# The first unit of the leading tiles by token halves, with two of five token blocks loaded behind the first conditioning and weights

## The chip, the core and the metric

The kernel runs on one core of a Trainium2 chip. The metric is the device time of one execution in microseconds. Before the change it is 2295.79 us, the median of three runs (2294.99, 2295.79 and 2299.85).

A core has a tensor engine (PE, with its weight loads shown as PEld), a vector engine (DVE), a scalar engine (ACT), GpSimd (POOL) and SyncE (SP), which here only issues transfers. Each engine runs its own instructions in the order in which they stand in its queue. Transfers between HBM and on-chip memory run on 16 DMA engines; most are issued by SP, the first four token tiles by ACT and the small rows by POOL.

## The reference

Two layers of a diffusion trunk are run for 512 latent tokens and 128 context tokens, 640 rows of width 2048 together. Each layer normalises its input, applies a shift and a scale per feature that come from a condition vector, projects the result, mixes, projects back and adds a gated residual. The part that the change touches is the start of the first layer:

```python
m = jax.nn.silu(cond) @ w + b                                # ada_w: 2048 x 6144 for each layer
y = xf * lax.rsqrt(jnp.mean(xf * xf, axis=-1, keepdims=True) + EPS)
hs = rms_norm(xs, norm_g[layer]) * (1.0 + sc_s) + sh_s       # latent tokens, condition c
hp = rms_norm(xp, norm_g[layer]) * (1.0 + sc_p) + sh_p       # context tokens, condition c_ctx
h @ w_in                                                     # 2048 x 6656 in the even layer
```

## The kernel before

Activations are kept with features on the 128 partitions and the 640 tokens along the free axis; `h` has 16 feature tiles. Each is held as a rounded part and a remainder (`hi`, `lo`), and each weight tile as `wh` and `wl`; a product is three matmuls (L256 to L258 of the profile): `wh*hi`, `wh*lo`, `wl*hi`. A matmul covers 320 tokens, one *token half* (`HV`): half 0 is tokens 0 to 319, half 1 is 320 to 639, whose last 128 are the context tokens.

**The start.** The tokens come as five blocks of 128 rows, each in two tiles `xb` of 1024 features (L101): blocks 0 and 1 through ACT's queue, blocks 2 to 4 through SP's. `x_block` (L878) transposes a block in four groups of four PE transposes (L884) into PSUM; DVE copies three of the groups and ACT the fourth into `xT` (L885), and ACT sums the squares of the block (L889). GpSimd takes the inverse root. `x_rows` (L895) spreads the inverse roots of the tokens over all partitions with one matmul a block (L899), and ACT copies them into `rows` (in `tables`, L900). Small rows (norm gains, biases, convolution weights, condition vectors) are loaded as `rows_a` and `rows_b` and turned by two transposes (L127, L128) into one PSUM tile; `sT`, the condition on partitions, is read from it. PSUM tiles for all of these come from two buffers (`psT`).

**Conditioning.** `ada_on_pe` (L163) computes two feature tiles of the shift or scale: two transfers of 1 MB (`ada`, L170, four buffers), 16 matmuls (L173), a copy on ACT (L176), two transposes (L179), a reduction on DVE (L181) and the bias (L161); a scale is then combined with the norm gain (L149).

**Leading tiles.** `run_tiles` begins with eight output tiles of the projection, the *leads*, while the conditioning still arrives. The inner dimension is taken in eight *units* of two feature tiles. A unit loads the weights of the eight leads (128 KB each, `load_raw`, L233, four buffers), rounds them on ACT (L220) and takes the remainder on DVE (L221), makes `h` (L922, then L926 on ACT and L927 on DVE) and runs 96 matmuls. Two leads keep their sum in PSUM through all units; the other six (`TRANS`) go through one pair of PSUM buffers and are copied (first unit, L349, ACT) or added (later, L351, DVE) into `sum`. After the first lead of a unit `ahead` issues the next unit's scale and shift.

The order in which the engines' instructions stand is set by a scheduler that starts from the program's order, and by the buffers of the pools: an instruction that needs a buffer waits for the last reader of what was in it.

Of the kernel before, what the change touches and what calls it, by code (L numbers as in the profile page):

```python
# [20 lines left out]
P = 128  # L21
D = 2048
KT = D // P
NS = 512
# [26 lines left out]
def trunk_kernel(ctx: ExitStack, tc: tile.TileContext, I: dict, O: dict):  # L51
# [12 lines left out]
    def psT():  # L64
        return pT.tile([P, 512], F32, tag="T", name="T")
# [37 lines left out]


    nc.sync.dma_start(rows_a[0:16, :], I["c"].rearrange("b (k p) -> (b k) p", p=P))
# [20 lines left out]
    t0 = psT()  # L126
    PE.transpose(t0[:, 0:112], rows_a[0:112, :], ident[0:112, 0:112])  # L127
    PE.transpose(t0[:, 128:205], rows_b[0:77, :], ident[0:77, 0:77])  # L128
    V.tensor_scalar(sT[:, :, 0:2], t0[:, 0:32].rearrange("p (c k) -> p k c", c=2), 0.5, None, ALU.mult)
    V.tensor_copy(vec[:, 0:80], t0[:, 32:112])  # L130
    V.tensor_copy(vec[:, 80:157], t0[:, 128:205])
    norm_g = [vec[:, 0:16], vec[:, 16:32]]
# [29 lines left out]

    def ada_on_pe(l, cb, h=0, n=4):  # L163

        acc, m, wd = psT(), 16 // n, n * P
        for kt in range(KT):
            if kt % m == 0:
                w = ada_t[0].rearrange("p (k n) -> p k n", k=m)
                ada_t.append(ada_t.pop(0))
                nc.sync.dma_start(w, I["ada_w"][l, kt * P:(kt + m) * P, cb * 512 + h * 256:cb * 512 + h * 256 + wd]  # L170
                                  .rearrange("(k p) n -> p k n", p=P))
            g = kt % 4
            PE.matmul(acc[32 * g:32 * g + 32, 0:wd], sT[:, kt, :], w[:, kt % m, :],  # L173
                      start=(kt < 4), stop=(kt >= KT - 4), tile_position=(0, 32 * g))
        sb = ada_sb
        A.copy(sb[:, 0:wd], acc[:, 0:wd])  # L176
# [131 lines left out]
    def slot(fill=None, rate=0.0, attend=True):  # L308
# [4 lines left out]
        while credit[0] >= 1.0:  # L313
            next(fill, None)
            credit[0] -= 1.0

    def run_tiles(jobs, w_ap, make_h, fill=None, rate=0.0, ahead=None, order=(0, 1, 2, 3), before=None,
                  last=None, by_half=False, mid=False, trans=[], grace=0, cut=None, summed=None, led=None, freed=None):
        if trans:
# [12 lines left out]
        units = [(pos, qd, js) for pos, qd in enumerate(order) for js in (cut or [(0, 4)])]  # L332
        for ui, (pos, qd, js) in enumerate(units):
            raws = {n: load_raw(w_ap, jobs[n][0], qd, js) for n in leads[:W_BUFS]}
            parts = {n: split_w(raws[n]) for n in raws}
# [537 lines left out]
    xT = [t[:, 0:4 * NT].rearrange("p (j t) -> p j t", j=4) for t in xTm]  # L873
    rx = sp.tile([P, 5], F32, name="rx")

    rows = tables[:, 0:NT]

    def x_block(b, ts):  # L878
        s4 = small.tile([P, 2], F32, tag="s4", name="s4")
        for g in range(4):  # L880
            ta = psT()
            for j in range(4):
                o = g % 2 * 512 + j * P
                PE.transpose(ta[:, j * P:(j + 1) * P], ts[g // 2][:, o:o + P], ident)  # L884
            (A.copy if g == 3 else V.tensor_copy)(xT[g][:, :, b * P:(b + 1) * P],  # L885
                                                  ta.rearrange("p (j t) -> p j t", j=4))
            if g % 2 == 0:
                junk = pS.tile([P, 1024], F32, tag="S", name="sqj")
# [29 lines left out]
    def h0_maker(k):  # L918
        x = xT[k // 4][:, k % 4, :]
        t = h_t[k % 2]  # L920
        for sl, c in TOKS:
            V.scalar_tensor_tensor(out=t[:, sl], in0=x[:, sl], scalar=gsc[0][:, k, c:c + 1], in1=rows[:, sl],  # L922
                                   op0=ALU.mult, op1=ALU.mult)
        hi, lo = new_h(k)
        for sl, c in TOKS:
            A.activation(hi[:, sl], t[:, sl], AF.Identity, bias=mod[0][:, k, c:c + 1])  # L926
# [131 lines left out]
    for i in range(4, 8):  # L1058
        b_tiles(i)

    u0, c0, b0, h0, g0, g1 = jobs[4:10]
    jobs[0:10] = [u0, c0, jobs[0], jobs[1], g0, jobs[2], jobs[3], g1, b0, h0]
    run_tiles(jobs, I["ev_w_in"][0], h0_maker, fill0, FILL0, ada_group, trans=TRANS, grace=GRACE, cut=((0, 2), (2, 4)),
              summed=keep, led=even_start, freed=ada_start)
    drain(prep)
# [604 lines left out]
```

## Time and profile before

| what | value |
|---|---|
| median of three runs | 2295.79 us |
| profiled execution, device time | 2294.4 us |
| its span, first to last instruction | 2292.6 us |
| PE busy | 2255.9 us (98%) |
| DVE / ACT / POOL busy | 1589.8 / 1088.9 / 160.0 us |
| bytes moved | 342.89 MB, mean 150 GB/s |
| granted clock of the tensor engine | 0.999 |

The page lists busy time by engine, then 40 slices of the span, the DMA queues, the chain of work that ended last, and groups of instructions by line with mean duration and the idle time ahead of them. Other views are instructions in order of time, waits, and the busy time of each engine in chosen stretches. An ended wait is put down to the signal that came last. Matmuls overlap: one of 320 columns is shown as 0.31 us, and the next begins 0.15 us after it.

### The profile page before, as it was taken

The numbers are of one execution on the slowest core, as the hardware profiler recorded it, in microseconds if no ns is written. First come the engines' busy times: TensorE is split into PE (matmuls) and PEld (weight loads), VectorE is DVE, ScalarE is ACT, GpSimd is POOL, SyncE is SP. The second block draws the span as 40 slices with busy tenths as digits, with TensorE's granted clock in tenths as the row PEclk, the third lists the DMA queues.
The fourth block names the chain that finished last, engine by engine and source line by source line (L and its number), as shares of the span: only waits on it lengthen the run. The fifth ranks groups of instructions, "written<-read, shape, count | busy, mean of one in ns | idle before, by whom it ended". The sixth has DMA issues, their size and how long they took to land.

```text
span 2292.6 us, 41100 instructions
## 1 busy us (share of the span) xinstructions
PE 2255.9 (98%) x15900; PEld 2178.0 (95%) x15900; DVE 1589.8 (69%) x2831; ACT 1088.9 (47%) x2304; POOL 160.0 (7%) x224
## 2 busy tenths in 40 slices
PE   7999999999999999999999999999999999999999
PEld 5889999999999999999999999999999999999999
DVE  4666968779779776887787665365665655557775
ACT  5325652443522222544464443465565676755443
POOL 1001000000000000000100001011111100000101
PEclk9999999999999999999999999999999999999999
DMA  9985537547367564854553335223223221238642
GB/s 321 294 270 161 158 113 218 152 133 219 116 210 216 177 191 137 277 173 140 164 155 108 116 118 152 79 60 104 79 63 101 71 60 49 76 101 269 184 138 62
DMA packets 380899, 342.89 MB, mean 150 GB/s; under 512 B 16402, under 2 KB 338416, under 8 KB 380192
## 3 DMA queue, kind: packets, MB, share of 16 engines
q1 hardware_dynamic: 366288, 296.00, 43.0%
q0 software_dynamic: 13696, 42.10, 5.4%
q8 instruction: 125, 2.05, 0.4%
q10 hardware_dynamic: 720, 2.16, 0.3%
q14 instruction: 70, 0.57, 0.1%
HBM read 301.27 MB, written 38.93 MB: 148 GB/s over the span
## 4 chain that ended last, share of the span: by engine, by line
PE 85%; DVE 4%; ACT 4%; DMA 3%; issue 3%; POOL 1%; SPq 0%; ACTq 0%; POOLq 0%; DVEq 0%
PE pq L537 7%; PE pq L536 7%; PE pq L535 7%; PE pa L256 6%; PE pa L257 6%; PE pb L256 6%; PE pa L258 6%; PE pb L257 6%; PE pb L258 6%; PE pb L271 2%; PE pb L270 2%; PE pa L270 2%; PE pb L272 2%; PE pa L272 2%; PE pa L271 2%
## 5 line engine op out<-in xcount | busy, mean ns | idle before, releaser
L220 ACT ACTIVATE wh<-raw 128x512 fp32r<-128x512 f32 (+1 forms) x456 | 273.1, 600 | 574.0 <-PE pb L257 406.9
L221 DVE TENSOR_TENSOR wl<-raw,wh 128x512 fp32r<-128x512 f32 (+1 forms) x456 | 295.7, 650 | 212.3 <-ACT wh L220 191.9
L256 PE MATMUL pa<-h,wh 128*128 128x320 f32 x1024 | 325.3, 319 | 4.3 <-ACT h L220 2.0
L257 PE MATMUL pa<-h,wh 128*128 128x320 f32 x1024 | 319.5, 313 | 1.7 <-DVE h L221 0.8
L258 PE MATMUL pa<-h,wl 128*128 128x320 f32 x1024 | 318.2, 311 | 0.9 <-DVE wl L221 0.9
L257 PE MATMUL pb<-h,wh 128*128 128x320 f32 x1024 | 317.1, 310 | 0.0
L258 PE MATMUL pb<-h,wl 128*128 128x320 f32 x1024 | 316.8, 309 | 0.0
L256 PE MATMUL pb<-h,wh 128*128 128x320 f32 x1024 | 316.6, 310 | 0.0
L198 DVE SCALAR_TENSOR_TENSOR acc<-adaw,sT,acc 128x1024 f32<-128x1024 f32 x240 | 299.7, 1276 | 0.0
L256 PEld LDWEIGHTS pa<-h,wh 128*128 128x128 f32 x1024 | 193.1, 189 | 18.3 <-issue 10.0
L257 PEld LDWEIGHTS pa<-h,wh 128*128 128x128 f32 x1024 | 193.3, 189 | 7.6 <-issue 3.3
L535 PE MATMUL pq<-h,wh 128*128 128x320 f32 x640 | 198.7, 311 | 0.4 <-ACT wh L220 0.4
L537 PE MATMUL pq<-h,wl 128*128 128x320 f32 x640 | 198.0, 309 | 0.1
L536 PE MATMUL pq<-h,wh 128*128 128x320 f32 x640 | 197.7, 309 | 0.0
L258 PEld LDWEIGHTS pa<-h,wl 128*128 128x128 f32 x1024 | 193.1, 189 | 3.5 <-issue 2.1
L257 PEld LDWEIGHTS pb<-h,wh 128*128 128x128 f32 x1024 | 192.2, 188 | 1.0 <-issue 0.8
L256 PEld LDWEIGHTS pb<-h,wh 128*128 128x128 f32 x1024 | 192.1, 188 | 0.8 <-issue 0.4
L258 PEld LDWEIGHTS pb<-h,wl 128*128 128x128 f32 x1024 | 192.3, 188 | 0.0
L537 PE MATMUL pq<-T,wl 128*128 128x320 f32 x480 | 147.7, 308 | 0.2 <-DVE wl L221 0.2
L536 PE MATMUL pq<-T,wh 128*128 128x320 f32 x480 | 147.9, 308 | 0.0
L535 PE MATMUL pq<-T,wh 128*128 128x320 f32 x480 | 147.6, 308 | 0.1
L270 PE MATMUL pa<-h,wh 128*128 128x320 f32 x432 | 141.0, 326 | 0.0
(431 smaller groups left out, 5306.0 us busy)
## 6 DMA issues: line engine op xcount, KB each, us to landing
adaw<-in_ada_w SPq DMA_DIRECT2D x128, 512.0 KB, 4.3
raw<-in_ev_w_in SPq DMA_DIRECT2D x176, 256.0 KB, 3.5
raw<-in_od_w_in SPq DMA_DIRECT2D x160, 256.0 KB, 2.9
ada<-in_ada_w SPq DMA_DIRECT2D x32, 1024.0 KB, 7.9
w<-in_od_w_in SPq DMA_DIRECT2D x24, 512.0 KB, 4.0
yd<-y POOLq DMA_DIRECT2D x32, 320.0 KB, 3.2
yin<-yd SPq DMA_DIRECT2D x32, 320.0 KB, 4.5
w<-yd SPq DMA_DIRECT2D x32, 320.0 KB, 4.2
```

The lines of the kernel that those rows point to most:

```text
L198: V.scalar_tensor_tensor(out=acc[c], in0=w, scalar=sT[:, kt, c:c + 1], in1=acc[c], op0=ALU.mult, op1=ALU.add)
L220: A.activation(hi, x, AF.Copy)
L221: V.tensor_sub(lo, x, hi)
L256: PE.matmul(ps, wh[:, i, :], hi[:, sl], start=(j == js[0] if alone else (pos == 0 and j == 0)), stop=False)
L257: PE.matmul(ps, wh[:, i, :], lo[:, sl], start=False, stop=False)
L258: last_mm[0] = PE.matmul(ps, wl[:, i, :], hi[:, sl], start=False, stop=(j == js[1] - 1 if alone else (pos == 3 and j == 3)))
L270: PE.matmul(ps, wh[:, j, :], hi[:, sl], start=(qd == 0 and j == 0), stop=False)
L271: PE.matmul(ps, wh[:, j, :], lo[:, sl], start=False, stop=False)
L272: PE.matmul(ps, wl[:, j, :], hi[:, sl], start=False, stop=(qd == 3 and j == 3))
L535: PE.matmul(ps, wh[:, j, :], hi, start=(new and h == 0 and j == 0), stop=False, **kw)
L536: PE.matmul(ps, wh[:, j, :], lo, start=False, stop=False, **kw)
L537: PE.matmul(ps, wl[:, j, :], hi, start=False, stop=(h == 1 and j == 3), **kw)
```

## The change

Four things are done.

- Only blocks 0 to 2 are loaded at the beginning. `first_loads` then issues the first unit's two scale tiles, the weights of leads one and two (both in one buffer, `first_raws`), the two shift tiles, the other six leads' weights in three buffers, and behind them blocks 3 and 4. It transposes blocks 0 to 2, computes scale, the norm rows of three blocks, and shift.
- `first_unit` runs the first unit by token halves: `h` of both feature tiles for half 0, the eight leads with 24 + 24 matmuls, then the same for half 1. The six leads with sums alternate between two PSUM buffers by their number, and each half is copied by ACT.
- `between` puts the transposes of block 3 behind the third lead of half 0, those of block 4 behind the sixth, `rows_b` behind the seventh, and the two missing norm rows behind the eighth. Squares of blocks 3 and 4 are taken in four quarters on ACT into an SBUF tile, as the PSUM tile that held them before is one of the leads' sums now. The block's transposes are held behind the last matmul ahead of them.
- The transpose of `rows_a` and `rows_b` is split: the 32 rows of the condition first, `rows_a` behind block 0, `rows_b` late.

The amount of data and of arithmetic stays, but for one transpose more and eight quarter squares in place of four.

```diff
-    xs = [x_load(b) for b in range(5)]
+    xs = [x_load(b) for b in range(3)]
...
-    PE.transpose(t0[:, 0:112], rows_a[0:112, :], ident[0:112, 0:112])
-    PE.transpose(t0[:, 128:205], rows_b[0:77, :], ident[0:77, 0:77])
+    PE.transpose(t0[:, 0:32], rows_a[0:32, :], ident[0:32, 0:32])
...
+    def first_unit(raws, leads, trans, pps, make_h, ahead, units, between):
+        pos, qd, js = units[0]
+        parts = {}
+        for i, raw in enumerate(raws):
+            wh, wl = split_w(raw)
+            for j in range(2):
+                parts[leads[2 * i + j]] = wh[:, j], wl[:, j]
+        for half_i, sl in HV:
+            for k in range(*js):
+                make_h(k, half_i)
+            for i, n in enumerate(leads):
+                if half_i and n == leads[1]:
+                    ahead(*units[1][1:])
+                if n in trans:
+                    pp = {half_i: pproj.tile([P, 512], F32, tag="p%s0" % "ab"[i % 2], name="pf")}
+                    proj_q(pp, parts[n], qd, pos, [(half_i, sl)], alone=True, js=js)
+                    A.copy(pps[n][half_i], pp[half_i][:, 0:HALF])
+                else:
+                    proj_q(pps[n], parts[n], qd, pos, [(half_i, sl)], js=js)
+                if not half_i:
+                    between(i)
...
+    def squares_of(b, ts):
+        s4 = small.tile([P, 4], F32, tag="s4", name="s4")
+        for g in range(4):
+            A.activation(sqj, ts[g // 2][:, g % 2 * 512:g % 2 * 512 + 512], AF.Square, accum_out=s4[:, g:g + 1])
+        return s4
...
-    for b in range(5):
-        x_block(b, xs[b])
-    ada_on_pe(0, 4, 0, 2)
-    x_rows((0, 1, 2, 3))
-    x_rows((4,))
-    ada_on_pe(0, 0, 0, 2)
+    def first_loads(cols):
+        scale = [ada_load(0, 4, kt, 0, 2) for kt in (0, 8)]
+        raws = [first_raws(I["ev_w_in"][0], cols[0:2], (0, 2))]
+        shift = [ada_load(0, 0, kt, 0, 2) for kt in (0, 8)]
+        raws += [first_raws(I["ev_w_in"][0], cols[i:i + 2], (0, 2)) for i in (2, 4, 6)]
+        xs.extend(x_load(b) for b in (3, 4))
+        x_block(0, xs[0])
+        vec_rows(0, 80, rows_a, 32)
+        x_block(1, xs[1])
+        x_block(2, xs[2])
+        ada_on_pe(0, 4, 0, 2, scale)
+        x_rows((0, 1, 2))
+        ada_on_pe(0, 0, 0, 2, shift)
+        return raws
+
+    def between(i):
+        if i in (2, 5):
+            b = 3 + i // 5
+            x_block(b, xs[b])
+        elif i == 6:
+            vec_rows(80, 77, rows_b, 0)
+        elif i == 7:
+            x_rows((3, 4))
```

How the instructions then stand is shown at three places. The first is ACT at the start: `xb_97` and `xb_99` are block 1's halves, `xb_101` and `xb_103` block 2's, `sqj` the squares and `xT3` the copy of a block's fourth group. Before:

```order
L889 ACTIVATE sqj_251,s4_244<-xb_97 128x1024
L889 ACTIVATE sqj_265,s4_244<-xb_99 128x1024
L885 COPY xT3_209<-T_234 128x4x128
L889 ACTIVATE sqj_284,s4_277<-xb_101 128x1024
L889 ACTIVATE sqj_298,s4_277<-xb_103 128x1024
L885 COPY xT3_209<-T_267 128x4x128
```

and now (`wh_393<-raw_203` rounds the first pair of weights, `raw_208`, `raw_211` and `raw_214` are the other three, `ada_sb` is the copy of a conditioning, first the scale's and then the shift's, and `h0_410` is the first `h`):

```order
L937 ACTIVATE sqj_301,s4_294<-xb_101 128x1024
L227 ACTIVATE wh_393<-raw_203 128x512
L937 ACTIVATE sqj_315,s4_294<-xb_103 128x1024
L933 COPY xT3_198<-T_284 128x4x128
L933 COPY xT3_198<-T_317 128x4x128
L183 COPY ada_sb_116<-T_327 128x256
L227 ACTIVATE wh_397<-raw_208 128x512
L948 COPY tables_136<-T_352 128x384
L227 ACTIVATE wh_401<-raw_211 128x512
L227 ACTIVATE wh_405<-raw_214 128x512
L183 COPY ada_sb_116<-T_357 128x256
L922 ACTIVATE sqj_200,s4_439<-xb_217 128x512
```

Weights are rounded between the squares and the copies of the blocks, and three roundings stand ahead of the shift's copy; the first quarter square of block 3 (`xb_217`) comes right behind it.

The second place is DVE at the same time (`xT0` to `xT2` are the copies of a block's first three groups; `T_276` is block 1's third, `T_295` to `T_309` are block 2's). Now:

```order
L933 COPY xT2_197<-T_276 128x4x128
L228 TENSOR_TENSOR wl_394<-raw_203,wh_393 128x512
L939 TENSOR_REDUCE ssx_323<-s4_294 128x1
L933 COPY xT0_195<-T_295 128x4x128
L940 TENSOR_SCALAR ssx_323<-ssx_323 128x1
L933 COPY xT1_196<-T_303 128x4x128
```

The remainder of the first pair of weights and the sum of block 2's squares stand ahead of the copies of block 2, where before no weight stood ahead of any block's copy.

The third place is PE inside the first unit, from the end of half 0 to the start of half 1 (`pf` is a lead's PSUM tile, `xb_223` block 4's second half, `rx` the inverse roots, `T_570` the second unit's scale). Now:

```order
L932 MATMUL T_517<-ident_78,xb_223 128x128 x4
L264 MATMUL pf_527<-h1_414,wh_405 128x320
L265 MATMUL pf_527<-h1_414,wl_406 128x320
L131 MATMUL T_535<-ident_78,rows_b_105 128x77
L263 MATMUL pf_538<-h0_410,wh_405 128x320
...
L265 MATMUL pf_538<-h1_414,wl_406 128x320
L947 MATMUL T_546<-ident_78,rx_199 128x128 x2
L180 MATMUL T_570<-ada0_112,sT_81 32x256 x8
L180 MATMUL T_570<-ada1_113,sT_81 32x256 x5
L263 MATMUL pf_562<-h0_410,wh_393 128x320
```

Before, the same stretch of PE held the last norm rows, the shift, and the first matmuls of both halves:

```order
L899 MATMUL T_409<-ident_78,rx_210 128x128
L173 MATMUL T_412<-ada2_122,sT_81 32x256 x8
L173 MATMUL T_412<-ada3_123,sT_81 32x256 x8
L179 MATMUL T_432<-ident_78,ada_sb_124 128x128 x2
L173 MATMUL T_504<-ada0_120,sT_81 32x256 x5
L256 MATMUL pa_488<-h0_476,wh_458 128x320
L256 MATMUL pb_489<-h0_476,wh_458 128x320
```

Transposes of two blocks and two norm-row matmuls moved from ahead of the first projection matmul to behind it, and between the halves stand thirteen matmuls of the second unit's conditioning. Behind the eight units of the leading tiles every engine's order is the same in both kernels.

More of the change, by code (lines that the diff above doesn't have):

```diff
@@ L315, in slot, with first_raws @@
             credit[0] -= 1.0
+    def first_raws(w_ap, cols, js):
+        raw = wpool.tile([P, 2, 2, P], F32, tag="raw", name="raw")
+        for i, col in enumerate(cols):
+            nc.sync.dma_start(raw[:, i], w_ap[js[0] * P:js[1] * P, col:col + P].rearrange("(k p) n -> p k n", p=P))
+        return raw
+    def first_unit(raws, leads, trans, pps, make_h, ahead, units, between):
[19 more added lines that the diff above has]
+                    between(i)
     def run_tiles(jobs, w_ap, make_h, fill=None, rate=0.0, ahead=None, order=(0, 1, 2, 3), before=None,
-                  last=None, by_half=False, mid=False, trans=[], grace=0, cut=None, summed=None, led=None, freed=None):
+                  last=None, by_half=False, mid=False, trans=[], grace=0, cut=None, summed=None, led=None, freed=None,
+                  first=None, between=None):
         if trans:
@@ L333, in run_tiles @@
         for ui, (pos, qd, js) in enumerate(units):
+            if first and ui == 0:
+                first_unit(first, leads, trans, pps, make_h, ahead, units, between)
+                continue
             raws = {n: load_raw(w_ap, jobs[n][0], qd, js) for n in leads[:W_BUFS]}
@@ L874, in trunk_kernel @@
     rx = sp.tile([P, 5], F32, name="rx")
+    sqj = sp.tile([P, 512], F32, name="sqj")
     rows = tables[:, 0:NT]
+    def squares_of(b, ts):
[3 more added lines that the diff above has]
+        return s4
     def x_block(b, ts):
-        s4 = small.tile([P, 2], F32, tag="s4", name="s4")
+        s4 = small.tile([P, 2], F32, tag="s4", name="s4") if b < 3 else squares_of(b, ts)
         for g in range(4):
             ta = psT()
-            for j in range(4):
-                o = g % 2 * 512 + j * P
-                PE.transpose(ta[:, j * P:(j + 1) * P], ts[g // 2][:, o:o + P], ident)
+            with tc.issue_after(last_mm[0].ins) if b > 2 else ExitStack():
+                for j in range(4):
+                    o = g % 2 * 512 + j * P
+                    PE.transpose(ta[:, j * P:(j + 1) * P], ts[g // 2][:, o:o + P], ident)
             (A.copy if g == 3 else V.tensor_copy)(xT[g][:, :, b * P:(b + 1) * P],
                                                   ta.rearrange("p (j t) -> p j t", j=4))
-            if g % 2 == 0:
+            if b < 3 and g % 2 == 0:
                 junk = pS.tile([P, 1024], F32, tag="S", name="sqj")
@@ L1062, in trunk_kernel @@
     jobs[0:10] = [u0, c0, jobs[0], jobs[1], g0, jobs[2], jobs[3], g1, b0, h0]
+    raws = first_loads([jobs[n][0] for n in (0, 2, 1, 3, 4, 5, 6, 7)])
     run_tiles(jobs, I["ev_w_in"][0], h0_maker, fill0, FILL0, ada_group, trans=TRANS, grace=GRACE, cut=((0, 2), (2, 4)),
-              summed=keep, led=even_start, freed=ada_start)
+              summed=keep, led=even_start, freed=ada_start, first=raws, between=between)
     drain(prep)
```

29 lines of the change are left out of this document (18 added, 11 removed).

## Prediction

> **What bounds the kernel now.** I read the page's totals and its chain first, then busy time by stretch, then the tensor engine (PE) in order of time.
>
> ```profile
> span 2292.6 us, 41100 instructions
> PE 2255.9 (98%) x15900; PEld 2178.0 (95%) x15900; DVE 1589.8 (69%) x2831; ACT 1088.9 (47%) x2304; POOL 160.0 (7%) x224
> PE 85%; DVE 4%; ACT 4%; DMA 3%; issue 3%; POOL 1%; SPq 0%; ACTq 0%; POOLq 0%; DVEq 0%
> ```
>
> The span is PE time. What the change can move is PE's idle time, and the next view shows where that is. Its columns are start:end, length, then busy time (and instructions) of PE, PEld, DVE, ACT, POOL, the granted clock, DMA share and GB/s.
>
> ```profile
> 0.00:12.40 12.40, 0.42 (x1) 0.20 (x2) 0.87 (x4) 4.93 (x8) 4.36 (x12) 1.00 0.83 286
> 12.40:27.90 15.50, 13.94 (x81) 9.74 (x81) 11.84 (x28) 10.09 (x19) 2.79 (x5) 1.00 1.07 373
> 27.90:36.50 8.60, 6.79 (x88) 3.84 (x88) 4.16 (x14) 4.18 (x11) 0.00 (x0) 1.00 1.06 336
> 36.50:56.40 19.90, 19.90 (x157) 16.15 (x157) 9.23 (x24) 10.13 (x27) 0.00 (x0) 1.00 0.93 294
> 56.40:110.00 53.60, 53.60 (x464) 45.00 (x463) 35.57 (x92) 17.04 (x41) 0.00 (x0) 1.00 0.91 288
> 110.00:164.00 54.00, 53.41 (x469) 45.60 (x468) 36.21 (x94) 16.54 (x40) 0.60 (x1) 1.00 0.88 286
> ```
>
> Before 36.5 us PE does preparation; from 36.5 us on it is full, to 164 us with 0.6 us missing. A time saved ahead of 36.5 us is therefore kept to the end, and a PE instruction that moves from ahead of 36.5 us to behind it is paid in full. Behind the first eight units (PE's first 800 instructions or so) all five engines have the same order in both kernels, so nothing else moves. The next rows are PE in order of time: start, length, line, operation.
>
> ```profile
> 12.42 0.36 PE L128 MATMUL T<-ident,rows_b 77*128 77x77 f32 x1 [4.28 <-DMA rows_b<-in_d_q_norm]
> 27.91 1.93 PE L173 MATMUL T<-ada,sT 128*32 128x256 f32 x32 [0.18 <-DVE xT L885]
> 30.61 1.28 PE L899 MATMUL T<-ident,rx 128*128 128x128 f32 x10
> 32.34 1.93 PE L173 MATMUL T<-ada,sT 128*32 128x256 f32 x32 [0.45 <-ACT tables L900]
> 35.57 1.02 PE L173 MATMUL T<-ada,sT 128*32 128x256 f32 x10 [0.31 <-DMA ada<-in_ada_w]
> 36.52 0.41 PE L256 MATMUL pa<-h,wh 128*128 128x320 f32 x1
> ...
> 52.16 0.62 PE L173 MATMUL T<-ada,sT 128*32 128x256 f32 x2
> ...
> 56.29 0.31 PE L258 MATMUL pb<-h,wl 128*128 128x320 f32 x1
> 56.44 0.31 PE L256 MATMUL pa<-h,wh 128*128 128x320 f32 x1
> ```
>
> The first unit's projection runs from 36.52 us, and the second unit's starts at 56.44 us (starts are 0.15 us apart). A matmul of L173 is two records, so 16 of them are the 1.93 us. The question is when the second unit can start in the changed kernel.
>
> **The change, part by part.** *The row transpose.* PE stood 4.28 us before L128 for the small rows, and the token blocks' transposes were behind it. They start after the 32-row transpose now, about 7 us. That removes up to 5 us ahead of the blocks, and L128's 0.36 us goes into the first half's matmuls.
>
> *When the first data are there.* The queue of SP gives the arrival times; the last line of each group is the time from issue to landing.
>
> ```profile
> L101 SPq DMA_DIRECT2D xb<-in_x_sample x1: 582/582/582, 2.8 to 2.8; - x1
> L101 ACTq DMA_DIRECT2D xb<-in_x_sample x1: 335/335/335, 3.2 to 3.2; - x1
> DMA to landing us min/median/max: 9.9/10.2/10.5
> ...
> L101 SPq DMA_DIRECT2D xb<-in_x_prompt x1: 328/328/328, 10.9 to 10.9; - x1
> DMA to landing us min/median/max: 7.4/7.4/7.4
> ...
> L170 SPq DMA_DIRECT2D ada<-in_ada_w x1: 435/435/435, 11.3 to 11.3; - x1
> DMA to landing us min/median/max: 10.0/10.0/10.0
> ```
>
> Blocks 1 and 2 land at about 13.3 us (2.8 + 10.5) and SP's share of the engines does not change ahead of that. The last token half lands at 18.3 us and the 1 MB conditioning tile queued behind it at 21.3 us: 3.0 us a megabyte with the queue full. In the changed order, from 13.3 us: the scale tiles at 16.3 and 19.3, the first weight pair (256 KB) at 20.05, the shift tiles at 23.05 and 26.05, the other three weight pairs at 26.8, 27.55 and 28.3, block 3 at 31.3, block 4 at 34.3, the second unit's four tiles at 37.3, 40.3, 43.3 and 46.3. So two blocks less ahead of the conditioning are 6 us of transfer, and the four early weight pairs take 3 us of them back.
>
> *Who waits in the queues.* ACT and DVE work in order, and the order shows three waits. ACT copies block 0's last group only behind both squares of block 1. On ACT the first pair's rounding (20.05 us) stands ahead of block 2's second square and of block 1's last copy; on DVE its remainder stands ahead of all of block 2's copies. And the rounding of pairs 2 to 4 stands ahead of the copy that the shift needs. These are the prices:
>
> ```profile
> L889 ACT ACTIVATE sqj<-xb 128x1024 f32<-128x1024 f32 x10 | 10.3, 1028 | 4.5 <-DMA xb<-in_x_sample 4.4
> L885 DVE COPY xT<-T 128x512 f32<-128x512 f32 x15 | 10.1, 690 | 2.9 <-PE T L884 2.6
> L885 ACT COPY xT<-T 128x512 f32<-128x512 f32 x5 | 2.9, 586 | 4.5 <-PE T L884 4.5
> L889 ACT ACTIVATION_READ_ACCUMULATOR sqj<-xb 128x1 f32 x10 | 1.9, 188 | 0.0
> L176 ACT COPY ada_sb<-T 128x256 f32<-128x256 f32 x2 | 0.7, 372 | 2.8 <-PE T L173 2.8
> ...
> L349 ACT COPY sum<-pa 128x320 f32<-128x320 f32 x6 | 2.5, 425 | 6.7 <-PE pa L258 6.7
> ...
> L221 DVE TENSOR_TENSOR wl<-raw,wh 128x512 fp32r<-128x512 f32 x49 | 33.6, 686 | 17.9 <-ACT wh L220 17.8
> L220 ACT ACTIVATE wh<-raw 128x512 fp32r<-128x512 f32 x50 | 31.6, 632 | 65.3 <-PE pb L257 63.7 <-DVE sum L351 1.1
> ```
>
> Step by step: 20.05 + 0.63 (rounding) + 1.2 (square) + 0.6 (copy) = 22.5 us until PE has a PSUM buffer for block 2's second group. Three more groups with two DVE copies of 0.69 between them: 24.5. The scale's matmuls, 1.93: 26.4. Its copy, transposes and additions and the three norm rows: 27.9; the shift's matmuls 1.93: 29.9. Copy, transposes, sum, add, on the way one remainder on DVE and a quarter square on ACT: first `h` at 31.3 and first projection matmul at 31.8 us. The other chain (last weight pair 28.3, two roundings, then the same copy) gives 31.4, so neither alone decides.
>
> To this comes the clock, which I take from the transposes:
>
> ```profile
> L884 PE MATMUL T<-ident,xb x80: 272/273/475, 12.6 to 27.5; 128*128 128x128 f32 x80
> 12.45 0.78 PEld L884 LDWEIGHTS T<-ident,xb 128*128 128x128 f32 x4
> 17.10 0.42 PEld L884 LDWEIGHTS T<-ident,xb 128*128 128x128 f32 x4 [0.29 <-ACT xT L885]
> ```
>
> After a pause of 4.28 us the transposes took 0.475 us each and a group's loads 0.78 us; about 4 us later 0.273 and 0.42. The granted clock column says 1.00 in both, so the durations decide. In the changed kernel PE has nothing from about 17.0 to 22.5 us, a longer pause, and block 2's groups and half of the scale's matmuls would run at the slow price: three groups 0.36 longer, half of it beside DVE's copies, and 0.7 on the matmuls (0.97 x 475/273), about 1.2 us. I take it: first projection matmul at 33.0 us, 3.5 us earlier than before.
>
> The Trainium skill, "TensorE: Matmul & The Clock Gate", section "What's actually happening", gives the rule: an idle window of some 3.4 us halves the clock and as long a busy one restores it. By that rule, with its free-running window, the sum below is +1.1 us or, if the pause misses a whole window, -0.1 us. The trace agrees in size (475 against 273 ns).
>
> *Inside the first unit.* Before, it took 56.44 - 36.52 = 19.9 us, with one matmul of the third unit's conditioning in it (0.5 until the next row goes on, at 52.16): 19.4. Added now: 5 conditioning matmuls that ran ahead of it before (10 records at 35.57; 5 x 0.12 = 0.6), eight groups of transposes at 0.42 (3.4), two norm-row matmuls (4 of the 10 records in 1.28: 0.5), the row transpose (0.1): 4.6 us.
>
> The waits inside are not shown by any row of before, so I bound them. The second half's `h` needs block 4's norm row, which ACT copies behind eight quarter squares (0.6 by the 512-wide copy and rounding, and 0.19 to read the sum: 6.4 us), six sum copies (0.42 each: 2.5), two block copies (1.2) and two `h` (0.9): 11 us from the first `h` on. PE's first half is 48 x 0.147 + 4.0 = 11 us as well. Both arrive together, and thirteen conditioning matmuls (landed by 40.3, PE there at about 45) fill 1.7 of the 2 us from norm row to `h`. From below the term is -0.6 (of the old 19.4 us, 96 x 0.147 + 28 x 0.12 + 0.4 = 17.9 are work, and a part of the other 1.5 may go), from above +3 (the norm row 1 us late and its 2 us uncovered). I take 0, near the lower end, because that cover is there by count. The body is 19.4 + 4.6 = 24.0 us.
>
> **Sum.** 33.0 + 24.0 = 57.0 us, against 36.5 + 19.4 = 55.9: the second unit is 1.1 us later, and with PE full behind it, so is the end. The profiled execution (2294.4 us, of which 2292.6 are span) becomes 2295.5; the median of the three runs, 2295.79, stands 1.4 us above it and becomes **2296.9 us**. What starts 3.5 us earlier pays it back in the 4.6 us that moved behind the start. The second unit's tiles land by 46.3 us, ten before its start, so DMA does not take over.
>
> **Rivals.** *A, the start comes much earlier.* If no weight pair held up ACT and DVE, the last shift tile at 26.05 us would decide: eight matmuls (1.0), then the 2.25 us that lay before from the shift's last matmul (32.34 + 1.93) to 36.52: first matmul at 29.3, second unit at 53.3, or 52.7 with the waits' lower bound: 2.6 to 3.2 us early, 2292.6 to 2293.2. For it: every transfer time above is an estimate, and a weight pair 2 us sooner frees block 2 by as much. Against: the order puts the rounding ahead. It passes 4.6 us only with the shift's tiles landing 1.5 us sooner too.
>
> *B, slower: SP's queue runs dry.* The fourth weight pair takes the first pair's buffer, which is free after DVE's remainder (20.05 + 0.63 + 0.69 = 21.4 us); behind it in SP's order stand blocks 3 and 4. If their issue slips until the last shift tile has landed, the pair comes 7.4 us (the shortest row above) after 26.05, at 33.5 in place of 28.3, and the first matmul at 36.6 in place of 33.0: +4.7 us, up to +5.7 with the blocks late as well: 2300.5 to 2301.5. It decides when the pair lands after 30 us. Against: at 21.4 us two shift tiles, 4.6 us of transfer, are still in flight.
>
> *C, the change does not do what it says.* The small rows' wait goes, but the first matmul stays near 35.5 us, because PE runs slow through the shift's matmuls too (another 1.2) and its copy waits for one more rounding or square on ACT (1.2): +3.6 us, 2299.4. For it: three chains meet there. Against: the two that I followed end within 0.4 us.
>
> **How the numbers follow.** A difference of 0.2% (4.6 us) is about what a measurement of this kernel can tell from no change; the three runs differ by 4.9. Forecast (second unit within 2 us of 57.0): 0.68. A: 0.14, of which 0.05 beyond 4.6 us. B: 0.10, all beyond. C: 0.08, of which 0.03 beyond. Faster 0.05, same 0.82, slower 0.13. The range, 2292.0 to 2301.5, reaches from A's end to B's and holds both bounds of the inner waits.
>
> **What would show it.** In the profile after: first projection matmul between 31.5 and 34 us; PE idle from about 17 to 22.5 us, ended by ACT's copy; slow transposes after it; the second unit's first matmul at 56 to 58 us and everything behind shifted by the same amount. I am wrong if block 2's transposes run before 19 us, if the first `h` waits for block 3, or if PE stands more than 3 us between the halves.

## The result, and the profile after

| | before | changed |
|---|---|---|
| median | 2296.26 us (20 runs) | 2300.61 us (20 runs) |
| lowest to highest | 2293.3 to 2302.5 us | 2294.7 to 2307.5 us |
| profiled execution, its span | 2294.4, 2292.6 us | 2299.26, 2297.5 us |
| granted clock, median over the runs | 0.998 | 0.9955 |

The ratio of the times is 1.0018, with a 95% interval from 1.0010 to 1.0026: slower by about 4 us, a little less than the 0.2% (4.6 us) that counts as no change here, but clear of zero. (The clock of before is that of 33 runs beside the first experiments.) The forecast was 2296.9 us in a range from 2292.0 to 2301.5.

The busy times by stretch of the changed kernel, with the same columns as in the prediction: to the second group of the second block's transposes, to the second group of the third block's, to the first projection matmul, to the second unit; the last row is a later stretch.

```profile
0.00:14.91 14.91, 4.81 (x23) 3.65 (x23) 3.96 (x14) 6.61 (x12) 5.01 (x14) 0.98 0.86 300
14.91:22.02 7.11, 3.48 (x16) 2.77 (x16) 3.01 (x6) 3.13 (x6) 0.49 (x1) 0.74 1.10 355
22.02:33.94 11.92, 9.81 (x86) 5.73 (x87) 5.48 (x15) 4.63 (x11) 0.55 (x1) 0.74 1.05 344
33.94:60.23 26.29, 26.29 (x203) 22.18 (x203) 14.20 (x37) 16.09 (x42) 1.10 (x2) 0.94 0.95 305
...
110.00:168.00 58.00, 55.00 (x472) 47.55 (x471) 37.13 (x95) 14.64 (x36) 0.60 (x1) 0.97 0.83 268
```

Two rows differ from what the prediction reckoned with. The first unit took 26.3 us instead of 24.0, with the granted clock at 0.94 in it. And the last row has 3 us of idle PE and a lower clock, far behind the start, where before only 0.6 us were missing. PE in order of time shows the first:

```profile
22.02 3.01 PE L932 MATMUL T<-ident,xb 128*128 128x128 f32 x12 [3.63 <-ACT xT L933]
24.97 3.45 PE L180 MATMUL T<-ada,sT 128*32 128x256 f32 x32
29.96 1.93 PE L180 MATMUL T<-ada,sT 128*32 128x256 f32 x32
33.94 0.41 PE L263 MATMUL pf<-h,wh 128*128 128x320 f32 x1 [1.06 <-ACT h L993]
...
34.79 0.33 PE L265 MATMUL pf<-h,wl 128*128 128x320 f32 x1
34.93 0.46 PE L263 MATMUL pf<-h,wh 128*128 128x320 f32 x1
...
38.12 0.41 PE L263 MATMUL pf<-h,wh 128*128 128x320 f32 x1
...
60.23 0.31 PE L263 MATMUL pa<-h,wh 128*128 128x320 f32 x1
```

The 32 records of the scale took 3.45 us where those of the shift took 1.93. From 34.93 to 38.12 us twelve projection matmuls stand 0.267 us apart instead of 0.147: (0.267 - 0.147) x 12 = 1.4 us. The second unit starts at 60.23 us, 3.8 us later than before.

The second loss is made by SP's queue. Its rows are start, time in which the issue held the queue, line, transfer and count; before first, and the changed kernel in the second fence:

```profile
136.65 0.38 SPq L170 DMA_DIRECT2D ada<-in_ada_w  x1
...
137.75 2.26 SPq L170 DMA_DIRECT2D ada<-in_ada_w  x2
144.04 2.72 SPq L233 DMA_DIRECT2D raw<-in_ev_w_in  x3
146.86 0.42 SPq L170 DMA_DIRECT2D ada<-in_ada_w  x1
147.33 1.73 SPq L68 DMA_DIRECT2D sink<-in_a_sink  x1
149.16 7.24 SPq L233 DMA_DIRECT2D raw<-in_ev_w_in  x5
```

```profile
140.54 5.80 SPq L169 DMA_DIRECT2D ada<-in_ada_w  x3
147.68 2.90 SPq L240 DMA_DIRECT2D raw<-in_ev_w_in  x3
150.67 1.11 SPq L169 DMA_DIRECT2D ada<-in_ada_w  x1
151.83 2.85 SPq L956 DMA_DIRECT2D band<-in_k_band  x1
154.74 0.42 SPq L68 DMA_DIRECT2D sink<-in_a_sink  x1
155.26 8.48 SPq L240 DMA_DIRECT2D raw<-in_ev_w_in  x5
```

The conditioning loads of the last unit (`ada`) start 3.9 us later than before, as the second unit did. But the band table's load, which stood ahead of them before (135.64 us), now stands behind the last one and holds the queue for 2.85 us, while the DMA engines are full (share 1.11 from 150 to 155 us). The weights behind it are issued at 155.26 us instead of 149.16: 6.1 us later, 2.3 more than the shift. ACT waits for them, DVE for ACT, and PE for the addition that stands behind it on DVE; then the clock falls too. ACT and DVE in order of time, in the changed kernel:

```profile
155.57 0.73 ACT L227 ACTIVATE wh<-raw 128x256 fp32r<-128x256 f32 x2 [4.43 <-DMA raw<-in_ev_w_in]
156.01 0.43 DVE L228 TENSOR_TENSOR wl<-raw,wh 128x256 fp32r<-128x256 f32 x1 [2.88 <-ACT wh L227]
```

PE's waits from 110 to 168 us (in total, times, longest; before, the longest was 0.6):

```profile
PE pa L263 <- DVE sum L391: 2.6, 1, 2.6
```

and the stretch from 155 to 160 us, with PE busy for 3.02 us at a granted clock of 0.78:

```profile
155.00:160.00 5.00, 3.02 (x14) 3.05 (x15) 2.18 (x6) 1.14 (x3) 0.00 (x0) 0.78 0.87 275
```

and the same stretch before:

```profile
155.00:160.00 5.00, 5.00 (x72) 2.91 (x72) 2.74 (x9) 0.80 (x3) 0.60 (x1) 1.00 0.69 268
```

Two places mark the two losses in every run below: DVE's first addition into the sums of unit 2 (57.52 us before, 61.31 changed: +3.8), and GpSimd's last write of `x0d`, behind the leading tiles (182.76 and 189.90 us: +7.1). So 3.8 us are lost in the start and 3.3 between the two places, around 155 us; at the end of this profiled pair 4.9 are left.

### The profile page after: what moved, and what is told of

Same layout as the page of the kernel before. It is cut to its first block, busy times and chain, and to the rows that moved or that the text cites. A ratio compares the mean times of both kernels' runs of the same rounds, so it can differ in the third digit from the quotient of the medians.

```text
span 2297.5 us, 41103 instructions
## 1 busy us (share of the span) xinstructions
PE 2259.5 (98%) x15901; PEld 2183.8 (95%) x15901; DVE 1591.1 (69%) x2831; ACT 1090.0 (47%) x2310; POOL 160.0 (7%) x224
## 4 chain that ended last, share of the span: by engine, by line
PE 87%; ACT 4%; DVE 4%; DMA 3%; issue 1%; SPq 0%; POOL 0%; ACTq 0%; DVEq 0%; POOLq 0%
PE pq L577 7%; PE pq L576 7%; PE pq L575 7%; PE pa L263 6%; PE pa L264 6%; PE pa L265 6%; PE pb L263 6%; PE pb L264 6%; PE pb L265 6%; PE pb L278 2%; PE pb L277 2%; PE pa L277 2%; PE pb L279 2%; PE pa L279 2%; PE pa L278 2%; PE T L775 2%
## 5 line engine op out<-in xcount | busy, mean ns | idle before, releaser
L264 PE MATMUL pb<-h,wh 128*128 128x320 f32 x1012 | 313.8, 310 | 0.0
L263 PE MATMUL pb<-h,wh 128*128 128x320 f32 x1012 | 313.1, 310 | 0.0
```

What stands on the lines that cost most here:

```text
L263: PE.matmul(ps, wh[:, i, :], hi[:, sl], start=(j == js[0] if alone else (pos == 0 and j == 0)), stop=False)
L264: PE.matmul(ps, wh[:, i, :], lo[:, sl], start=False, stop=False)
```

## The experiments

"Of before" below is always against the kernel before on the same chip (medians 2296.4, 2297.7 and 2297.5 us for runs 1 to 4, 5 to 8, 9 to 12). Each run was also timed in five rounds, 11 or 12 executions.

| run | edit | first addition, unit 2 | last write of x0d | median, against before | ratio, 95% interval |
|---|---|---|---|---|---|
| before | | 57.52 | 182.76 | | |
| changed | | 61.31 | 189.90 | +4.4 us | 1.0018 (1.0010 to 1.0026) |
| 1 | before, small rows later | 56.66 | 183.48 | -4.0 | 0.9986 (0.9975 to 0.9997) |
| 2 | changed, PE kept busy | 61.02 | 191.61 | +6.6 | 1.0022 (1.0013 to 1.0031) |
| 3 | changed, rounding later | 58.78 | 189.12 | +2.5 | 1.0010 (1.0001 to 1.0019) |
| 4 | changed, band and sink early | 58.66 | 184.39 | +0.7 | 1.0000 (0.9991 to 1.0009) |
| 5 | before, band late | 57.59 | 183.30 | -1.5 | 0.9998 (0.9988 to 1.0008) |
| 6 | 3 and 4, squares later | 57.73 | 182.79 | -2.7 | 0.9990 (0.9980 to 1.0001) |
| 7 | 6, PE kept busy | 59.81 | 184.79 | -1.3 | 0.9998 (0.9988 to 1.0007) |
| 8 | 1 again | 56.18 | 181.31 | -2.6 | 0.9987 (0.9978 to 0.9997) |
| 9 | 10, PE kept busy | 55.41 | 180.99 | -2.0 | 0.9992 (0.9983 to 1.0001) |
| 10 | 6, two roundings behind `h` | 57.00 | 183.97 | -0.8 | 0.9995 (0.9986 to 1.0004) |
| 11 | 10, small loads late | 55.43 | 183.21 | +0.5 | 1.0000 (0.9991 to 1.0009) |
| 12 | changed, again | 58.94 | 190.65 | +3.4 | 1.0015 (1.0006 to 1.0024) |

### Run 12: the changed kernel again

> The changed kernel itself once more, unedited, to see what of its start is fixed and what varies. Theory (the two slow spells of the start depend on the moment, the orders do not): first projection matmul between 32.8 and 34, where the spells fall differs or one is missing, the stall near 155 us is there again, median 2298.5 to 2301.5. Rival (all of it is fixed): the same first matmul and the same two spells within 0.3 us.

PE in order of time:

```profile
25.21 2.36 PE L180 MATMUL T<-ada,sT 128*32 128x256 f32 x32
...
33.10 0.41 PE L263 MATMUL pf<-h,wh 128*128 128x320 f32 x1 [1.06 <-ACT h L993]
...
34.40 0.31 PE L265 MATMUL pf<-h,wl 128*128 128x320 f32 x1
```

Its stretch from 155 to 160 us:

```profile
155.00:160.00 5.00, 3.52 (x13) 3.55 (x14) 2.05 (x5) 0.96 (x3) 0.00 (x0) 0.58 0.55 162
```

The slow spell of the projection is missing in this execution, and the scale was slow for part of its matmuls only: first projection matmul at 33.1 us, unit 2 only 1.4 us later than before. The stall is there again, and larger: ACT waits 5.67 us for its weights, and x0d is 7.9 us later. So of the two losses the start's varies with the clock (1.4 and 3.8 us in two profiles), and the stall stays.

### Runs 4 and 5: the small loads around the last conditioning

Run 4 puts the band's load and the sink row's ahead of the conditioning loads, in the changed kernel:

```diff
-        for cb in (4 + g, g):
-            ada_on_pe(0, cb, js[0] // 2, js[1] - js[0])
...
+            load_rows(sink, "a_sink")
+            bd = nc.sync.dma_start(band, I["k_band"])
+        with tc.issue_after(bd.ins) if last else ExitStack():
+            for cb in (4 + g, g):
+                ada_on_pe(0, cb, js[0] // 2, js[1] - js[0])
```

> The changed kernel with one thing moved on SP's queue: the loads of the band table (192 KB) and of the sink row are issued ahead of the last unit's first conditioning load instead of behind its last one. Theory (the band load, moved by the change from a slack place to the place right ahead of unit 7's second weights, holds the queue for 2.85 us): the PE stall and the dip of the granted clock between 153 and 162 us shrink or go, and the whole is 2.5 to 3.3 us under the changed kernel, near 2297.5. Rival (the stall comes from the conditioning loads that are themselves late): the stall stays, the time stays at 2300.6 or grows.

SP's queue in run 4:

```profile
138.31 0.47 SPq L68 DMA_DIRECT2D sink<-in_a_sink  x1
138.83 0.43 SPq L956 DMA_DIRECT2D band<-in_k_band  x1
139.35 1.00 SPq L169 DMA_DIRECT2D ada<-in_ada_w  x2
...
150.04 8.47 SPq L240 DMA_DIRECT2D raw<-in_ev_w_in  x5
```

The weights are issued at 150.04 us, 5.2 us sooner than in the changed kernel and 4.7 sooner than in run 12 (154.77), though unit 2 began only 0.3 us sooner than there. From first addition to x0d it loses 0.5 us against before, where the changed kernel lost 3.3 and 6.5. The closest comparison is run 3 below, which leaves these loads where the changed kernel has them and begins unit 2 only 0.12 us later than run 4:

```profile
150.14 2.79 SPq L963 DMA_DIRECT2D band<-in_k_band  x1
...
153.50 9.46 SPq L240 DMA_DIRECT2D raw<-in_ev_w_in  x5
```

Its weights are issued 3.5 us later than run 4's, and it loses 5.1 us between the two marks; run 2, with the same order, loses 5.4. The median of run 4 is 3.5 us under the changed kernel (2297.08 against 2300.61); taken each against its own before, it is 2.7 to 3.7 us. The theory holds in place and about in size. One thing moved with it that was not meant to: the third conditioning load now stands behind two of the next weights. No run separates that from the place of the two small loads.

Run 5 is the reverse on the kernel before: `with tc.issue_after(last_ada[0].ins):` around the band's load.

> The reverse of the run before it, on the kernel before: its only edit pins the band table's load (192 KB) on SP behind the last unit's fourth conditioning load, which is where the changed kernel has it; nothing else differs from the kernel before but the sink row's load, which moves up one place. Theory (the place of that one load is most of the loss): PE stalls between 148 and 158 us as in the changed kernel, and the whole is 2.5 to 3.5 us above the kernel before, near 2299.4. Rival (the loss belongs to the start, and the stall in the changed kernel to its own order of weights): within 1 us of the kernel before.

SP's queue in run 5:

```profile
146.82 0.42 SPq L172 DMA_DIRECT2D ada<-in_ada_w  x1
147.29 2.23 SPq L911 DMA_DIRECT2D band<-in_k_band  x1
149.62 7.31 SPq L235 DMA_DIRECT2D raw<-in_ev_w_in  x5
```

Hardly a loss: the weights behind it are issued 0.46 us later than before (149.16), since the sink's load in that place held the queue for 1.73 us already. PE's waits from 110 to 190 us grow from 0.6 to 2.3 us, but x0d is only 0.5 us later and the median no higher. The theory that the band's place alone does it falls. What differs in the changed kernel is a second small load in that place, three conditioning loads of 1 MB in one row, and more of them still under way when the fourth is issued at 150.67 us: two, which land at 152.2 and 155.2 us, where before it was one, landing at 149.5. Which of these counts is not shown.

### Run 11: the same place with the start repaired

Run 10 without the edit of run 4; three small loads then stand behind the fourth conditioning load.

> The previous run's kernel with the small loads of the last group (third gain row, band table, sink row) left behind its fourth conditioning load on SP, as the changed kernel has band and sink. The start is the same. Theory (the loss near 155 us is made by SP's order there, not by the late start): unit 2 begins as in the previous run, but the last write of x0d falls 3 to 5 us later than there, PE waits over 2 us between 148 and 160, and the median is 2.5 to 4 us above it. Rival (it needs the later start, as the kernel before with only the band late showed no loss): within 1 us.

SP's queue in run 11:

```profile
145.71 0.56 SPq L169 DMA_DIRECT2D ada<-in_ada_w  x1
146.32 3.25 SPq L68 DMA_DIRECT2D gain_rows<-in_d_k_norm  x1
149.62 0.42 SPq L970 DMA_DIRECT2D band<-in_k_band  x1
150.09 0.43 SPq L68 DMA_DIRECT2D sink<-in_a_sink  x1
150.62 6.49 SPq L240 DMA_DIRECT2D raw<-in_ev_w_in  x5
```

In run 10 the five weight loads start at 149.62 us with unit 2 beginning 1.6 us later than here, so the order costs 2.6 us of issue. PE waits 2.9 us once, and against before 2.5 us are lost between the two marks. But run 10 loses 1.7 there too, so only 0.8 us of it are the order's, and x0d comes 0.8 us sooner than in run 10, not 3 to 5 later as expected. The median is 1.3 us above run 10, half of the least that was expected, and the intervals of the two overlap. So the expectation failed: without a late start the order costs little. With unit 2 about 1.2 us late, in runs 3 and 4, it cost 4.6 us between the marks.

### Runs 2 and 7: PE kept busy, and what spoiled it

Run 2 adds 40 transposes of the identity to the changed kernel (`keep_busy(last_tr[0], 26)`, and 5 and 9 more behind the shift).

> The changed kernel with 40 transposes of the identity added that nothing reads: 26 between blocks 1 and 2, 5 behind the shift matmuls, 9 behind the shift transposes, where PE stands idle. They leave no work out. Theory (a slowed TensorE clock after idle PE costs part of the start): the scale matmuls take about 1.9 us for 3.45, the projection matmuls from 34.9 to 38.1 stand 0.147 us apart instead of 0.267, the second unit begins 2.5 to 3 us earlier than at 60.2, and the whole is 2.5 to 3 us under the changed kernel. Rival (the clock does not matter there, or the start waits for loads): the second unit and the whole move by less than 0.5 us.

The scale took 1.93 us, as expected, and no projection matmul stood 0.267 us apart. But the scheduler put other work ahead on ACT. Two roundings, the second waiting for its transfer to 27.59 us, stood ahead of the copy of the scale's sums (28.13 us), and squares of block 3 ahead of the first `h`. PE stood for 2.08 us ahead of the scale's transposes, and the slow spell came there: the norm rows took 1.49 us instead of 0.83, and the shift slowed as well (1.93 in the changed kernel):

```profile
30.42 2.68 PE L182 MATMUL T<-ada,sT 128*32 128x256 f32 x32
```

The first projection matmul came at 35.43 us instead of 33.94, which took back the whole gain, and the stall at SP's queue was larger (4.5 us of PE waits). As a test of the time it failed.

Run 7 adds 49 such transposes to run 6, whose orders on ACT and DVE are pinned.

> The same as the run with all orders mended, and 49 transposes of the identity that nothing reads, in PE's gaps of the start: 22 in block 1, 6 behind block 2, 4 behind the scale matmuls, 7 behind the shift matmuls, 10 behind the shift transposes. ACT and DVE keep their order. Theory (gaps on PE bring the slowed clock): the granted clock stays at 0.95 or more in every 5 us from 10 to 45, and the median is 1 to 2 us under the run without them. Rival (the slowed clock comes whatever PE does there): the clock dips as often and the times are equal within 0.5 us.

ACT and PE of run 7 in order of time:

```profile
31.43 0.63 ACT L238 ACTIVATE wh<-raw 128x512 fp32r<-128x512 f32 x1 [2.55 <-DMA raw<-in_ev_w_in]
...
32.57 0.41 PE L274 MATMUL pf<-h,wh 128*128 128x320 f32 x1 [2.74 <-ACT h L1019]
...
34.65 0.47 PE L274 MATMUL pa<-h,wh 128*128 128x320 f32 x1
```

The clock stood at 1.00 from 10 to 30 us. Then the fourth weight pair came late (SP's order had changed, and it was issued behind block 3's tiles), its rounding stood on ACT ahead of `h`, PE stood for 2.74 us, and a slow spell came about 1.6 us behind the gap. The median is 1.5 us above run 6 instead of 1 to 2 under it.

### Runs 3 and 6: head-of-line waiting on ACT

Run 3 pins the roundings of the changed kernel's first unit: `with tc.issue_after(pa.ins), tc.issue_after(pd.ins): wh, wl = split_w(raw)`, where `pa` and `pd` are block 2's last copies for two pairs, and the shift's copy and sum for the others.

> The changed kernel with the rounding of the first unit's weights pinned behind block 2's copies (first two pairs) and behind the copy of the shift sums (last two pairs) on ACT and DVE. Theory (the weight pair that stands ahead of block 2's copies on ACT holds PE from 18.4 to 22.0): block 2 is done near 20, the shift matmuls start as their tiles land, the first projection matmul comes at 29.5 to 30 instead of 33.9, the second unit and the whole are 3.5 to 4 us earlier than in the changed kernel. Rival (the shift tiles land no earlier than 29 us): block 2 is done earlier but the shift matmuls still start near 29.5, and the whole gains under 1 us.

PE and ACT of run 3 in order of time:

```profile
21.38 1.93 PE L180 MATMUL T<-ada,sT 128*32 128x256 f32 x32
...
30.45 0.63 ACT L925 ACTIVATE sqj<-xb 128x512 f32<-128x512 f32 x1 [1.59 <-DMA xb<-in_x_sample]
...
31.67 0.63 PE L264 MATMUL pf<-h,wh 128*128 128x320 f32 x1 [3.37 <-ACT h L1001]
```

The scale starts 3.6 us sooner, so the wait on ACT was real. But the first matmul came at 31.67 us, since a square of block 3 stands on ACT ahead of the first `h` and waits for its transfer to 30.45 us: behind one head of the queue stood the next.

Run 6 pins the squares behind the first `h` as well, the second pair behind the scale, and takes run 4's edit.

> The changed kernel with the band table's load early, the first unit's roundings pinned behind block 2's copies (first pair), the scale group (second pair) and the shift group (last two), and the squares of block 3 pinned behind the first unit's h. Theory (what is left of the loss is head-of-line waiting on ACT): the first projection matmul comes at 29.3 to 30.2 instead of 32.8, the second unit at 55 to 55.5 instead of 57.6, and the whole is 2 to 3 us under the run with the band alone, near 2294.5. Rival (the start is given back by a slower clock or by a queue behind it): second unit no earlier than 57, time near 2297.

The first projection matmul came at 30.00 us, as expected, 3.9 sooner than in the changed kernel. But unit 2 starts at 56.65 us instead of 55 to 55.5: from 31.1 to 33.9 us the matmuls stand 0.267 us apart. The median, 2294.98, is 2.7 us under its own before, where run 4 was 0.7 above, with an interval that just reaches 1.

### Runs 9 and 10: the gap, and the gap filled

Run 10 is run 6 with pairs 3 and 4 pinned behind `h`; run 9 is the same with the 49 transposes.

> All orders mended as before, the roundings of pairs 3 and 4 now pinned behind the first unit's h, and the same 49 transposes that nothing reads in PE's gaps. Theory (a gap on PE of over a microsecond brings a slowed clock of about 3 us a little later, and a filled gap does not): no projection matmuls 0.267 us apart before 45 us, first projection matmul near 29.7, first addition into the sums of unit 2 at 55.5 to 56.2. Rival (the slowed clock comes anyway): a spell of 0.267 us spacing within the first 5 us of the projections, addition at 57 or later.

> The same without the added transposes. Theory of the gaps: first projection matmul near 29.7 as well, then a spell of 2.5 to 3.5 us of matmuls 0.267 us apart, first addition into unit 2's sums 1.2 to 1.7 us later than with the added transposes (57 to 57.7), median 1 to 2 us above it. Rival (clock independent of the gaps): the two agree within 0.5 us in both.

PE in order of time, run 9 first and run 10 in the second fence:

```profile
29.70 0.41 PE L274 MATMUL pf<-h,wh 128*128 128x320 f32 x1 [0.23 <-ACT h L1025]
...
31.27 0.31 PE L276 MATMUL pa<-h,wl 128*128 128x320 f32 x1
```

```profile
29.64 0.41 PE L264 MATMUL pf<-h,wh 128*128 128x320 f32 x1 [1.45 <-ACT h L1011]
...
31.31 0.47 PE L266 MATMUL pa<-h,wl 128*128 128x320 f32 x1
...
34.24 0.43 PE L265 MATMUL pf<-h,wh 128*128 128x320 f32 x1
```

The same start, 0.06 us apart. With the gap of 1.45 us a spell of about 3.2 us follows (granted clock from 30 to 35 us 0.66, and 1.00 in run 9), and unit 2's first addition comes 1.6 us later (57.00 against 55.41). The medians differ by 1.2 us (2296.65 and 2295.49), which their intervals do not separate, and SP's order differs too: run 9 issues the fourth weight pair behind block 3's tiles. This agrees with the theory of the gaps, with one reserve: run 11, without the transposes, has the same first matmul as run 10 (29.61) and the same gap of 1.45 us, and no spell behind it in its profile (55.43). A gap allows the spell and does not force it; that the transposes prevented it rests on this one pair of profiles.

### Runs 1 and 8: one part of the change alone

On the kernel before, only `rows_b`'s transpose and copy move behind the x blocks:

```diff
-    PE.transpose(t0[:, 128:205], rows_b[0:77, :], ident[0:77, 0:77])
...
+    t1b = psT()
+    PE.transpose(t1b[:, 0:77], rows_b[0:77, :], ident[0:77, 0:77])
+    V.tensor_copy(vec[:, 80:157], t1b[:, 0:77])
```

> One part of the change alone, on the kernel before: only the transpose of the late small rows (rows_b) and its copy stand behind the five x blocks, everything else is the kernel before. Theory (the small rows, which land last, hold the first x blocks back): the x transposes start at about 7.8 us instead of 12.4, the last block is done about 2 us earlier (25.8 for 27.9), the first projection matmul comes at about 34.4 for 36.5, and the whole is about 2 us under the kernel before. Rival (blocks 3 and 4 land too late for that to count): first projection matmul stays near 36.5 and the time is that of the kernel before.

> The kernel of the first run once more (only the late small rows moved behind the x blocks, on the kernel before), since its profile was of one of its slower executions (2296.5 beside a median of 2292.5). Theory (x blocks released early): first projection matmul 1.5 to 2 us before the 36.5 of the kernel before where the clock stays up, median near 2292.5. Rival (chance): the median falls back to that of the kernel before.

The medians are 4.0 and 2.6 us under before, with both intervals below 1: this version is faster than before, though by less than the 0.2% that counts as no change here. The way there is not the expected one. The x blocks do start at 8.5 and 9.1 us instead of 12.6, but the first projection matmul comes no sooner (36.97 and 36.47 us), because the last block and ACT's copy of the norm rows still decide. What is won is that eight conditioning matmuls of the next unit, not five, now run ahead of it; the first addition of unit 2 is 0.9 and 1.3 us sooner. That is less than the medians gained, and what gives the rest is open.

## Why the prediction was right or wrong

The time lies within 0.2% of before and in the range, 3.7 us above the forecast (2300.6 for 2296.9). That it is still in the range is luck: the upper part of the range was there for rival B, which did not happen, and what filled it was a loss some 120 us behind the start, for which the sum had no term. By its own steps:

- *When the data are there*: right. The first pair was rounded from 19.83 us on (20.05 forecast), and run 3 began to round its second pair at 26.54 us (26.8). In run 11 PE waited for the second shift tile to 25.79 us (26.05).
- *Who waits in the queues*: right. PE stood to 22.02 us behind ACT's copy, as forecast (22.5), and slow transposes followed. Run 3 removed that wait and the scale started 3.6 us sooner.
- *The clock*: the mechanism was right and the size was off. The 1.2 us ahead of the first matmul were 1.5 (3.45 for 1.93 us) in the scale alone, but only 0.4 in run 12 and nothing in run 4, at about the same pause; the second spell, 1.4 us in the first half, was not in the sum at all. First projection matmul: 33.0 forecast, 33.94 in this profile, 32.81 in run 4 and 33.10 in run 12.
- *Inside the first unit*: 24.0 us forecast, 26.3 in this profile. Without the spell it was 57.58 - 32.81 = 24.8 in run 4, so the sum of what moved there was 0.8 us short and the rest was clock. The waits between the halves stayed within their bounds.
- *The second unit*: 57.0 us was forecast, 1.1 later than the 55.9 that it took for before. In run 4, without the spell, it starts at 57.58, 1.1 us behind the 56.44 of before. In this profile it was 3.8.
- *"With PE full behind it, so is the end"*, and *"everything behind shifted by the same amount"*: this step failed. Behind the start the loss grew by 3.3 us here and 6.5 in run 12. SP's order had changed within the first eight units, and only what lies behind those was compared. The step rested on "so nothing else moves". Run 4 shows that moving the loads there takes most of the loss back, at a median 3.5 us lower (0.7 us above before). "DMA does not take over" held for unit 2 and not for unit 7, whose weights came late.
- *The rivals*: B had the right kind of mechanism, a queue of SP that delivers weights too late, but at the start, where it did not happen in the changed kernel (in run 7 something like it did: the fourth pair came at 31.43 us and the first matmul at 32.57). That the measured 2300.6 lies in B's 2300.5 to 2301.5 says nothing for it. A was not reached: the rounding did stand ahead of block 2, and when runs 6 and 10 took that away, the first matmul came at 30.0 and 29.6 us (29.3 in A), yet the second unit came at 56.65 us in run 6 instead of 53.3, since the first unit took 26.7 us, with a slow spell, and not 24.0. In run 9, without a spell, it came at 54.33, 1.0 us behind A. C did not happen: the shift's matmuls took 1.93 us and the first matmul came at 33.94, not near 35.5.
- *Saved time is kept*: run 9 supports it. Its first addition is 2.1 us sooner than before and its x0d 1.8 sooner.

Open: in the first profiled pair the difference falls from 7.1 us at x0d to 4.9 at the end, where nothing was changed. And the runs show that the order near 155 us and a late start make the stall together, but not which of the moved loads does it.

## What to carry to other kernels

When a change moves the time at which a stage starts, compare the issue order of the transfer queue for as long as the kernel still loads under a full DMA, not only around the edit: one small load that slips behind a megabyte cost next to nothing in one order (run 5) and, with others, about 3 us in another. In an in-order queue, look behind the head for the next one: runs 3 and 7 each had another late transfer waiting there. And a gap on PE is priced twice, once for its length and once for a possible slow spell behind it, here 1.4 us.

## What was not expected of the hardware

In four profiles the slow spells begin only 1.0 to 1.6 us after PE is full again (at 34.93 us where the gap ended at 33.94, at 31.07 where it ended at 29.64, and in runs 6 and 7); behind the gaps of run 2 (2.08 us) and run 3 (3.37) PE was slow at once. Those four last about 2.8 to 3.4 us, with matmuls 0.267 us apart instead of 0.147. A gap of 1.06 us brought one in the changed kernel's first profile and not in runs 12 and 4, and a gap of 1.45 us in runs 6 and 10 and not in run 11. The length and the chance agree with a free-running window of some 3.4 us, as the Trainium skill has it ("TensorE: Matmul & The Clock Gate", section "What's actually happening"). That page speaks of an idle window; here PE had worked for a part of the time, about 1.9 us of the shift's matmuls in the 4 us ahead of 33.94, and fell back all the same. Where the windows lie, no trace here shows.
